# Feed-forward activations transposed by the DMA crossbar as two 16-bit planes instead of by TensorE

## Chip, cores and metric

The kernel runs on one core of a Trainium2 chip. The metric is the device time of one launch in microseconds, the median of several runs. The core has five engines that each take their own instructions in order: TensorE (PE, with its weight loads shown as PEld), VectorE (DVE), ScalarE (ACT), GpSimd (POOL) and SyncE (SP). Sixteen DMA engines move data beside them; in the kernel before, all weight loads are issued from SP.

## What is computed

Two layers of a decoder trunk (sequence 256, model width 2048, float32). Each layer has an attention mixer with an input and an output projection, and then a gated feed-forward block. Only the last matters here:

```python
def swiglu(xn, w_gate, w_up, w_down):
    return (jax.nn.silu(xn @ w_gate) * (xn @ w_up)) @ w_down   # 2048 -> 5632 -> 2048

# per layer
xn = rms_norm(h, norm_ffn[layer])
h = h + swiglu(xn, w_gate[layer], w_up[layer], w_down[layer])
```

## The kernel before

**Precision.** A float32 product is made from three float32r products: each operand is split into a high part (a copy rounded to float32r) and a low part (the rest), and `mm` runs the passes high x high, low x high, high x low, for two row tiles of 128 tokens each.

**Items.** The weights stream through as a list of items, 402 for each layer. Nearly every item is a 128 x 1024 float32 tile (512 KB): two k-steps of 128 rows by 512 columns. In the feed-forward block an item is 2 k-steps x 3 passes x 2 row tiles = 12 matmuls of 512 columns. For an item, SP loads `raw`, ACT copies it to `hi`, DVE subtracts to get `lo`. There are five `raw` buffers and four each of `hi` and `lo`. In the loop, item i first runs `step(active)` (one step of every live side task, a Python generator that issues some instructions and yields), then `prefetch(i)`, which issues the split of item i+3 and the loads up to five items beyond it, and then the matmuls of item i. So the order of instructions on each engine is written out by this loop: whatever a side task issues in its k-th step stands ahead of the split of that turn.

**Feed-forward order.** The hidden width is cut into 11 chunks of 512 columns. The first part takes chunks 0 to 5, the second chunks 6 to 10. For each chunk come 8 items of `w_gate` (`g`) and 8 of `w_up` (`u`). After the `g` items `silu` runs as a side task, after the `u` items `gated`. When the chunks of a part are done, four `w_down` groups (`d0` to `d3`) multiply the transposed activations of that part: 12 items each in the first part, 10 in the second. The items of a group take the chunks in order, two items for each chunk, so in the second part the last chunk, 10, is first used by the ninth item of `d0`; in the first part chunk 5 is first used by the eleventh.

**The side task `gated`.** Counting from the last `u` item of the chunk, its steps fall in the turns of the following items, called item 1, item 2 and so on here. Step 1 (DVE) multiplies the silu tile `sil` by the second accumulator. Steps 2 and 3, one row tile each, run four TensorE transposes of 128 x 128 into a PSUM tile, a copy on ACT to `ah` (high part) and a subtraction on DVE to `al` (low part). Then the pair is put into `act[c]`, from which the `w_down` matmuls take their stationary operand. If the loop comes to a matmul whose `act[c]` isn't set yet, it runs further steps at once, behind the split of that turn:

```python
src = act if it.mat == "w_down" else XF
for kt in it.kts:
    while src[kt // 4] is None:
        step(active)
mm(pos, accs, lambda kt: src[kt // 4])
```

Of the kernel before, what the change touches and what calls it, by code (L numbers as in the profile page):

```python
# [6 lines left out]

F32 = mybir.dt.float32
F32R = mybir.dt.float32r
I32 = mybir.dt.int32  # L10
AF = mybir.ActivationFunctionType
OP = mybir.AluOpType
AX = mybir.AxisListType.X

P = 128
D = 2048
S = 256
# [104 lines left out]
def trunk(ctx: ExitStack, tc: tile.TileContext, x, positions, cst, gT, gfin, bgate, posT, w2, ws, out):  # L122
    nc = tc.nc
    V, A, T = nc.vector, nc.scalar, nc.tensor
# [14 lines left out]
    def tmp_ps():  # L139
        return ps.tile([P, 512], F32, tag="t", name="tps", bufs=3)  # L140
# [18 lines left out]
    def split_next():  # L159
        i = ptr[1]  # L160
        n = seq[i][1].n
        r = raw.pop(i)
        hi, lo = places[i]() if i in places else (wp.tile([P, 1024], F32R, tag="hi", name="hi", bufs=4),
                                                  wp.tile([P, 1024], F32R, tag="lo", name="lo", bufs=4))
        A.activation(hi[:, :n], r[:, :n], AF.Copy)  # L165
# [41 lines left out]
    w2t = cp.tile([P, DEPTH, 2, 2, P], F32, name="w2t")  # L207
    posi = cp.tile([P, 3], I32, name="posi")
    h = hp.tile([P, 2, D], F32, name="h")

    ident = cs[:, C_ID:C_ID + P]
# [150 lines left out]
    def xt_alloc(X, c):  # L362
        X[c] = (xp.tile([P, 4, S], F32R, tag="xh", name="xh", bufs=5),
                xp.tile([P, 4, S], F32R, tag="xl", name="xl", bufs=5))

# [74 lines left out]
    for l in range(DEPTH):  # L440
        g_mix, g_grp, g_ffn = gt[:, 3 * l, :], gt[:, 3 * l + 1, :], gt[:, 3 * l + 2, :]
        flags.clear()
        with ExitStack() as actx:
# [44 lines left out]
            def c_chunk(which, accs):  # L488
# [28 lines left out]
                while which == "cv" and "wk" not in flags:  # L517
                    yield
                fr = ap.tile([P, 32, 60], F32R, tag="fr", name="fr", bufs=1)
                for a in range(2):  # L520
# [293 lines left out]
            while seq[pos][1].mat in ("w_in", "w_cmp_k1", "w_cmp_v1"):  # L814
# [9 lines left out]
                if it.mat == "w_in":  # L824
# [14 lines left out]
                    if it.name == "sv1" and it.kts[-1] in (3, 7, 11):  # L839
                        c = it.kts[-1] // 4  # L840
# [34 lines left out]
            while seq[pos][1].mat == "w_out":  # L875
# [12 lines left out]
                c = int(it.name[1])  # L888
# [9 lines left out]
        with ExitStack() as fctx:  # L898
            fp = fctx.enter_context(tc.tile_pool(name=f"fp{l}", bufs=1))
            r = norm.r  # L900
            act = [None] * NFF
            sil = {}
# [8 lines left out]
                yield  # L911

            def gated(c, accs):
                for t in range(2):
                    s = sil[c, t]
                    V.scalar_tensor_tensor(s, accs[t], r[:, t:t + 1], s, op0=OP.mult, op1=OP.mult)  # L916
                yield
                ah = fp.tile([P, 4, S], F32R, tag="ah", name="ah", bufs=6)
                al = fp.tile([P, 4, S], F32R, tag="al", name="al", bufs=6)
                for t in range(2):  # L920
                    s = sil[c, t]
                    pt = tmp_ps()
                    for j in range(4):
                        T.transpose(pt[:, j * P:(j + 1) * P], s[:, j * P:(j + 1) * P], ident)  # L924
                    sl = slice(t * P, t * P + P)
                    pv = pt.rearrange("p (a b) -> p a b", a=4)
                    A.activation(ah[:, :, sl], pv, AF.Copy)  # L927
                    V.tensor_tensor(al[:, :, sl], pv, ah[:, :, sl].bitcast(F32), op=OP.subtract)  # L928
                    yield
                act[c] = (ah, al)  # L930

            last = l == DEPTH - 1
# [36 lines left out]
            while pos < (end_at if last else len(seq)) and seq[pos][1].mat in ("w_gate", "w_up", "w_down"):  # L969
                it = seq[pos][1]  # L970
                step(active)
                prefetch(pos)
                if it.first:
                    accs = [acc(), acc()]
# [5 lines that stand above are left out]
                if it.last:  # L980
                    c = int(it.name[1:])
                    if it.mat == "w_down":
                        end = it.k1 == KFF
                        spawn(d_add(accs, c, end, norm))
                        if end and not last:
                            spawn(xt_gen(X, c, lambda t, c=c: h[:, t, quad(c)], gt[:, 3 * (l + 1), :], f"d{c}"))
                    else:
                        spawn(silu(c, accs) if it.mat == "w_gate" else gated(c, accs))
                parts.pop(pos)
                pos += 1  # L990
# [94 lines left out]
```

## Time and profile before

| | us |
|---|---|
| median of 3 runs (2310.41 to 2310.79) | 2310.58 |
| the profiled execution's own time | 2310.39 |
| its span from first to last instruction | 2308.6 |
| TensorE busy in the span | 2290.6 |
| DVE busy | 1330.4 |
| ACT busy | 1078.9 |

The profiled execution's time is its span and 1.8 us around it. Busy time of TensorE counts a matmul from its start to its modelled end, and successive matmuls overlap; what a matmul costs in the stream is read from the distance between starts.

### The profile page before, as it was taken

Reading aid. Unit: us, or ns where it says so; the run is one execution under the profiler, and the core shown is the slowest. Engines: PE = TensorE matmul, PEld = TensorE weight load, DVE = VectorE, ACT = ScalarE, POOL = GpSimd, SP = SyncE. Lnnn points to the kernel's source line nnn. Section 1 sums busy time; section 2 is a strip of 40 time slices with the busy share of each in tenths; the row PEclk is TensorE's granted clock in tenths of the full one; section 3 lists DMA queues with packets and bytes.
Section 4 is the critical chain, followed back from the end, with each engine's and each line's share of the span. In section 5 each row is a group of like instructions: output and inputs, shape, how many; then the busy total and the mean of one; then the engine's idle time right before and its main releaser. Section 6 shows DMA issues by size and latency. Waiting matters only on the chain.

```text
span 2308.6 us, 28280 instructions
## 1 busy us (share of the span) xinstructions
PE 2290.6 (99%) x10842; PEld 1906.9 (83%) x10842; DVE 1330.4 (58%) x1766; ACT 1078.9 (47%) x1405; POOL 28.7 (1%) x59
## 2 busy tenths in 40 slices
PE   8999999999999999999999999999999999999998
PEld 7888888888888888888888888888888888888886
DVE  6766776655445445445567667765544544444554
ACT  6645554544444344444455455544444433444443
POOL 4000000000000000000000000000000000000000
PEclk9999999999999999999999999999999999999999
DMA  7854456566666666666567434456556565555653
GB/s 250 277 169 128 128 156 198 181 187 190 189 192 190 194 192 184 192 191 189 178 215 252 147 133 142 157 187 206 186 186 196 183 196 196 186 192 189 190 191 137
DMA packets 118824, 428.46 MB, mean 186 GB/s; under 512 B 13424, under 2 KB 13840, under 8 KB 118560
## 3 DMA queue, kind: packets, MB, share of 16 engines
q1 hardware_dynamic: 118464, 426.58, 58.3%
q8 instruction: 85, 1.39, 0.2%
q14 instruction: 51, 0.42, 0.0%
q0 software_dynamic: 224, 0.07, 0.0%
HBM read 424.50 MB, written 2.10 MB: 185 GB/s over the span
## 4 chain that ended last, share of the span: by engine, by line
PE 98%; DVE 1%; ACT 1%; DMA 0%; SPq 0%; issue 0%; ACTq 0%
PE acc L408 90%; PE ops L669 1%; PE tps L640 1%; PE tps L924 1%; PE tps L373 1%; PE ops L538 1%; PE ops L539 1%; PE tps L615 1%; PE tps L661 0%; PE ops L796 0%; DMA h<-in_x_dram 0%; PE tps L763 0%; PE ops L703 0%; PE tps L678 0%; DVE c L772 0%; DVE lo L166 0%
## 5 line engine op out<-in xcount | busy, mean ns | idle before, releaser
L166 DVE TENSOR_TENSOR lo<-raw,hi 128x1024 fp32r<-128x1024 f32 (+1 forms) x798 | 970.2, 1220 | 782.2 <-ACT hi L165 778.6
L165 ACT ACTIVATE hi<-raw 128x1024 fp32r<-128x1024 f32 (+1 forms) x798 | 836.2, 1054 | 779.7 <-PE acc L408 768.0
L408 PE MATMUL acc<-hi,xh 128*128 128x512 f32 (+2 forms) x2432 | 758.6, 393 | 0.0
L408 PE MATMUL acc<-hi,xl 128*128 128x512 f32 (+2 forms) x2432 | 739.2, 385 | 0.0
L408 PE MATMUL acc<-lo,xh 128*128 128x512 f32 (+2 forms) x2432 | 737.2, 384 | 0.0
L408 PEld LDWEIGHTS acc<-lo,xh 128*128 128x128 f32 x2432 | 453.2, 188 | 92.9 <-DVE lo L166 0.2
L408 PEld LDWEIGHTS acc<-hi,xl 128*128 128x128 f32 x2432 | 453.3, 188 | 92.4
L408 PEld LDWEIGHTS acc<-hi,xh 128*128 128x128 f32 x2432 | 442.6, 189 | 84.3 <-issue 6.7
L408 PE MATMUL acc<-hi,ah 128*128 128x512 f32 x680 | 211.6, 391 | 0.0
L408 PE MATMUL acc<-hi,al 128*128 128x512 f32 x680 | 210.8, 389 | 0.0
L408 PE MATMUL acc<-lo,ah 128*128 128x512 f32 x680 | 210.7, 389 | 0.0
L408 PEld LDWEIGHTS acc<-lo,ah 128*128 128x128 f32 x680 | 127.7, 188 | 26.7
L408 PEld LDWEIGHTS acc<-hi,al 128*128 128x128 f32 x680 | 127.6, 188 | 26.6
L408 PEld LDWEIGHTS acc<-hi,ah 128*128 128x128 f32 x680 | 126.8, 188 | 25.6
L927 ACT ACTIVATE ah<-tps 128x512 fp32r<-128x512 f32 x44 | 26.3, 598 | 92.3 <-PE tps L924 92.3
L928 DVE TENSOR_TENSOR al<-tps,ah 128x512 fp32r<-128x512 f32 x44 | 30.4, 691 | 54.8 <-ACT ah L927 54.8
L380 ACT ACTIVATE xh<-scr 128x512 fp32r<-128x512 f32 x48 | 29.2, 630 | 44.4 <-DVE scr L375 44.4
L909 ACT ACTIVATE sil<-acc,nr 128x512 f32<-128x512 f32 x44 | 27.9, 686 | 38.9 <-PE acc L408 38.9
L663 ACT ACTIVATE pT<-tps 128x256 f32<-128x256 f32 (+1 forms) x32 | 15.7, 491 | 63.2 <-PE tps L661 63.2
L375 DVE TENSOR_TENSOR scr<-tps,gt 128x512 f32<-128x512 f32 x48 | 30.9, 684 | 23.3 <-PE tps L373 23.3
L916 DVE SCALAR_TENSOR_TENSOR sil<-acc,nr,sil 128x512 f32<-128x512 f32 x44 | 31.0, 747 | 13.9 <-PE acc L408 13.9
L383 DVE TENSOR_TENSOR xl<-scr,xh 128x512 fp32r<-128x512 f32 x48 | 31.3, 692 | 5.0 <-ACT xh L380 2.9
(197 smaller groups left out, 976.0 us busy)
## 6 DMA issues: line engine op xcount, KB each, us to landing
raw<-in_ws_dram SPq DMA_DIRECT2D x792, 512.0 KB, 4.1
raw<-in_ws_dram SPq DMA_DIRECT2D x10, 420.0 KB, 4.8
h<-in_x_dram SPq DMA_DIRECT2D x3, 512.0 KB, 8.2
gf<-in_gfin_dram SPq DMA_DIRECT2D x1, 1024.0 KB, 6.6
out_dram<-h SPq DMA_DIRECT2D x4, 256.0 KB, 2.3
out_dram<-h SPq DMA_DIRECT2D x2, 512.0 KB, 3.1
cs<-in_cst_dram SPq DMA_DIRECT2D x1, 802.0 KB, 5.8
h<-in_x_dram SPq DMA_DIRECT2D x2, 256.0 KB, 4.0
```

The costliest lines, as they stand in the source:

```text
L165: A.activation(hi[:, :n], r[:, :n], AF.Copy)
L166: V.tensor_tensor(lo[:, :n], r[:, :n], hi[:, :n].bitcast(F32), op=OP.subtract)
L373: T.transpose(pt[:, j * P:(j + 1) * P], src[:, j * P:(j + 1) * P], ident)
L375: V.tensor_tensor(tv, pt.rearrange("p (a b) -> p a b", a=4), g[:, 4 * c:4 * c + 4, None].to_broadcast([P, 4, P]), op=OP.mult)
L380: A.activation(xh[:, :, t * P:t * P + P], ts[t], AF.Copy)
L383: V.tensor_tensor(xl[:, :, sl], ts[t], xh[:, :, sl].bitcast(F32), op=OP.subtract)
L408: T.matmul(accs[t][:, :it.w], x_[:, kt % 4, t * P:t * P + P], w_[:, sl], start=(kt == it.k0 and n == 0), stop=(kt == it.k1 - 1 and n == 2))
L538: T.matmul(o[:60, :256], fr[:, kt, :], hi[:, sl], start=(kt == 0), stop=False)
L909: A.activation(s, accs[t], AF.Silu, scale=r[:, t:t + 1])
L916: V.scalar_tensor_tensor(s, accs[t], r[:, t:t + 1], s, op0=OP.mult, op1=OP.mult)
L927: A.activation(ah[:, :, sl], pv, AF.Copy)
L928: V.tensor_tensor(al[:, :, sl], pv, ah[:, :, sl].bitcast(F32), op=OP.subtract)
```

## The change

The four TensorE transposes per row tile go, and with them the PSUM tile. Instead ACT takes each float32 tile apart into its two 16-bit halves (`pl`, 128 x 1024 of uint16 for each row tile), one transposing DMA issued from ACT moves all of `pl` (128 x 2048 of uint16, 512 KB, as sixteen 128 x 128 blocks) into `plt`, ACT puts the halves together again in `sT` by four copies, and then one ACT copy and one DVE subtraction of 128 x 1024 make `ah` and `al`. `pl`, `plt` and `sT` have one buffer each. The task has 10 yields where it had 3.

```diff
             def gated(c, accs):
                 for t in range(2):
                     s = sil[c, t]
                     V.scalar_tensor_tensor(s, accs[t], r[:, t:t + 1], s, op0=OP.mult, op1=OP.mult)
                 yield
+                pl = fp.tile([P, 2, 2, 512], U16, tag="pl", name="pl", bufs=1)
+                for t in range(2):
+                    A.activation(pl[:, t], sil[c, t].bitcast(U16).rearrange("p (n b) -> p b n", b=2), AF.Copy)
+                    yield
+                pt = fp.tile([P, 2, 2, 512], U16, tag="plt", name="plt", bufs=1)
+                nc.scalar.dma_start(pt.rearrange("p t b (a s) -> p (t b a) s", a=4),
+                                    pl.rearrange("p t b n -> p (t b n)"), transpose=True)
+                for _ in range(4):
+                    yield
+                f = fp.tile([P, 4, S], F32, tag="sT", name="sT", bufs=1)
+                fv = f.rearrange("p a s -> p (a s)").bitcast(U16).rearrange("p (a t s b) -> p t b a s", a=4, t=2, b=2)
+                for t in range(2):
+                    for b in range(2):
+                        A.activation(fv[:, t, b], pt[:, t, b].rearrange("p (a s) -> p a s", a=4), AF.Copy)
+                    yield
                 ah = fp.tile([P, 4, S], F32R, tag="ah", name="ah", bufs=6)
                 al = fp.tile([P, 4, S], F32R, tag="al", name="al", bufs=6)
-                for t in range(2):
-                    s = sil[c, t]
-                    pt = tmp_ps()
-                    for j in range(4):
-                        T.transpose(pt[:, j * P:(j + 1) * P], s[:, j * P:(j + 1) * P], ident)
-                    sl = slice(t * P, t * P + P)
-                    pv = pt.rearrange("p (a b) -> p a b", a=4)
-                    A.activation(ah[:, :, sl], pv, AF.Copy)
-                    V.tensor_tensor(al[:, :, sl], pv, ah[:, :, sl].bitcast(F32), op=OP.subtract)
-                    yield
+                A.activation(ah, f, AF.Copy)
+                V.tensor_tensor(al, f, ah.bitcast(F32), op=OP.subtract)
+                yield
                 act[c] = (ah, al)
```

Every line number of the kernel rises by 1 ahead of this place and by 11 behind it.

On ACT, around the first chunk of layer 0, before (`hi<-raw` is the split of an item, `sil<-acc,nr` the silu of a chunk, x9 means nine in a row):

```order
L909 ACTIVATE sil<-acc,nr 128x512 x2
L165 ACTIVATE hi<-raw 128x1024 x9
L927 ACTIVATE ah<-tps 128x4x128
L165 ACTIVATE hi<-raw 128x1024
L927 ACTIVATE ah<-tps 128x4x128
L165 ACTIVATE hi<-raw 128x1024 x6
L909 ACTIVATE sil<-acc,nr 128x512 x2
```

And the same place now:

```order
L910 ACTIVATE sil<-acc,nr 128x512 x2
L166 ACTIVATE hi<-raw 128x1024 x9
L923 ACTIVATE pl<-sil 128x1024
L166 ACTIVATE hi<-raw 128x1024
L923 ACTIVATE pl<-sil 128x1024
L166 ACTIVATE hi<-raw 128x1024
L926 DMA_TRANSPOSE plt<-pl 128x16x128
L166 ACTIVATE hi<-raw 128x1024 x4
L934 ACTIVATE sT<-plt 128x4x128 x2
L166 ACTIVATE hi<-raw 128x1024
L934 ACTIVATE sT<-plt 128x4x128 x2
L910 ACTIVATE sil<-acc,nr 128x512 x2
```

The two short copies have become two long ones, a DMA issue, and, four splits later, two pairs of short ones; the `ah` copy follows after one more split, behind the next chunk's silu.

Around the last chunk (10) of layer 0, ACT now has, with buffer numbers (`hi_8376` is the split of the item that first needs chunk 10, `hi_8435` that of the item three later):

```order
L166 ACTIVATE hi_8376<-raw_8283 128x1024
L166 ACTIVATE hi_8394<-raw_8305 128x1024
L934 ACTIVATE sT_8412<-plt_8338 128x4x128 x2
L166 ACTIVATE hi_8415<-raw_8324 128x1024
L934 ACTIVATE sT_8412<-plt_8338 128x4x128 x2
L166 ACTIVATE hi_8435<-raw_8344 128x1024
L938 ACTIVATE ah_8441<-sT_8412 128x1024
L166 ACTIVATE hi_8457<-raw_8362 128x1024
```

On PE the matmuls at the border between the item before and that item now read:

```order
L409 MATMUL acc_8285<-lo_8359,ah_8147 128x512
L409 MATMUL acc_8286<-lo_8359,ah_8147 128x512
L409 MATMUL acc_8285<-hi_8376,ah_8441 128x512
L409 MATMUL acc_8286<-hi_8376,ah_8441 128x512
L409 MATMUL acc_8285<-hi_8376,al_8442 128x512
L409 MATMUL acc_8286<-hi_8376,al_8442 128x512
```

And on DVE the subtractions around `al` of that chunk:

```order
L167 TENSOR_TENSOR lo_8416<-raw_8324,hi_8415 128x1024
L167 TENSOR_TENSOR lo_8436<-raw_8344,hi_8435 128x1024
L939 TENSOR_TENSOR al_8442<-sT_8412,ah_8441 128x1024
L167 TENSOR_TENSOR lo_8458<-raw_8362,hi_8457 128x1024
```

So `ah` and `al` of chunk 10 stand behind the split `hi_8435`/`lo_8436`, which is issued in the same turn as the matmuls that need them.

## Rows read from the trace of the kernel before

**Rows 1.** The page: span, busy time by engine, the chain that ended last.

```profile
span 2308.6 us, 28280 instructions
PE 2290.6 (99%) x10842; PEld 1906.9 (83%) x10842; DVE 1330.4 (58%) x1766; ACT 1078.9 (47%) x1405; POOL 28.7 (1%) x59
...
PE 98%; DVE 1%; ACT 1%; DMA 0%; SPq 0%; issue 0%; ACTq 0%
PE acc L408 90%; PE ops L669 1%; PE tps L640 1%; PE tps L924 1%; PE tps L373 1%; PE ops L538 1%; PE ops L539 1%; PE tps L615 1%; PE tps L661 0%; PE ops L796 0%; DMA h<-in_x_dram 0%; PE tps L763 0%; PE ops L703 0%; PE tps L678 0%; DVE c L772 0%; DVE lo L166 0%
```

**Rows 2.** Groups by line: busy us, mean ns of one, idle before and releaser.

```profile
L166 DVE TENSOR_TENSOR lo<-raw,hi 128x1024 fp32r<-128x1024 f32 (+1 forms) x798 | 970.2, 1220 | 782.2 <-ACT hi L165 778.6
L165 ACT ACTIVATE hi<-raw 128x1024 fp32r<-128x1024 f32 (+1 forms) x798 | 836.2, 1054 | 779.7 <-PE acc L408 768.0 <-DMA raw<-in_ws_dram 4.4 <-PE ops L538 2.3
...
L408 PEld LDWEIGHTS acc<-hi,ah 128*128 128x128 f32 x680 | 126.8, 188 | 25.6
...
L380 ACT ACTIVATE xh<-scr 128x512 fp32r<-128x512 f32 x48 | 29.2, 630 | 44.4 <-DVE scr L375 44.4
...
L927 ACT ACTIVATE ah<-tps 128x512 fp32r<-128x512 f32 x44 | 26.3, 598 | 92.3 <-PE tps L924 92.3
L924 PE MATMUL tps<-cs,sil 128*128 128x128 f32 x176 | 26.3, 272 | 0.0
```

**Rows 3.** Timeline of PE around chunk 0, layer 0: start, us, instruction.

```profile
473.66 0.60 PE L924 MATMUL tps<-cs,sil 128*128 128x128 f32 x4
474.01 0.70 PE L408 MATMUL acc<-hi,xh 128*128 128x512 f32 x2
474.55 0.63 PE L408 MATMUL acc<-hi,xl 128*128 128x512 f32 x2
...
476.85 0.60 PE L924 MATMUL tps<-cs,sil 128*128 128x128 f32 x4
```

**Rows 4.** Timeline of ACT, chunks 9 and 10 of layer 0; brackets: idle before.

```profile
1005.17 0.60 ACT L927 ACTIVATE ah<-tps 128x512 fp32r<-128x512 f32 x1 [2.55 <-PE tps L924]
...
1018.84 1.06 ACT L165 ACTIVATE hi<-raw 128x1024 fp32r<-128x1024 f32 x1 [1.66 <-PE acc L408]
1021.56 1.06 ACT L165 ACTIVATE hi<-raw 128x1024 fp32r<-128x1024 f32 x1 [1.66 <-PE acc L408]
1024.51 1.27 ACT L909 ACTIVATE sil<-acc,nr 128x512 f32<-128x512 f32 x2 [1.89 <-PE acc L408]
...
1049.65 0.60 ACT L927 ACTIVATE ah<-tps 128x512 fp32r<-128x512 f32 x1 [2.55 <-PE tps L924]
```

**Rows 5.** Timelines of ACT, DVE and PE where `d0` reaches chunk 10, layer 0.

```profile
1068.76 1.06 ACT L165 ACTIVATE hi<-raw 128x1024 fp32r<-128x1024 f32 x1 [1.66 <-PE acc L408]
...
1069.86 1.23 DVE L166 TENSOR_TENSOR lo<-raw,hi 128x1024 fp32r<-128x1024 f32 x1 [1.50 <-ACT hi L165]
...
1069.02 0.62 PE L408 MATMUL acc<-hi,ah 128*128 128x512 f32 x2
1069.47 0.61 PE L408 MATMUL acc<-hi,al 128*128 128x512 f32 x2
1069.92 0.62 PE L408 MATMUL acc<-lo,ah 128*128 128x512 f32 x2
```

**Rows 6.** The page: DMA queue (last: share of 16 engines); issues, KB, us to landing.

```profile
q1 hardware_dynamic: 118464, 426.58, 58.3%
...
raw<-in_ws_dram SPq DMA_DIRECT2D x792, 512.0 KB, 4.1
...
out_dram<-h SPq DMA_DIRECT2D x2, 512.0 KB, 3.1
...
gt<-in_gT_dram SPq DMA_DIRECT2D x1, 48.0 KB, 2.9
```

**Rows 7.** Windows after the last matmul: busy us by engine, granted clock, DMA share, GB/s.

```profile
2302.00:2304.00 2.00, 0.00 (x0) 0.00 (x0) 1.72 (x6) 1.20 (x3) 0.00 (x0) 1.00 0.00 0
2304.00:2306.00 2.00, 0.00 (x0) 0.00 (x0) 0.06 (x1) 0.25 (x1) 0.00 (x0) 0.72 0.89 342
```

More of the change, by code (lines that the diff above doesn't have):

```diff
@@ L9 @@
 F32R = mybir.dt.float32r
+U16 = mybir.dt.uint16
 I32 = mybir.dt.int32
```

## Prediction

> **What bounds the kernel.** I began with the page: TensorE is busy for 99% of the span, and the chain that ended last lies on it for 98% [rows 1]. The next question is whether anything else is near. The groups by line say no: ACT's splits take 1.05 us each and stood idle for 768 us in all until a matmul freed their buffer, and DVE's subtractions waited for ACT [rows 2]. So the weights are always split well ahead, and a change pays one for one if it takes time out of TensorE's stream, and costs nothing on ACT or DVE until it makes TensorE wait.
>
> How much ahead, the timeline shows. One feed-forward item lasts 2.72 us (the distance of two splits, 1018.84 to 1021.56) [rows 4]; in each, ACT works 1.06 us and idles 1.66. The split that runs as item k starts is for item k+3; it begins 0.26 us ahead of item k's first matmul (1068.76 against 1069.02) [rows 5].
>
> **What goes.** Four transposes: from the start of one such group to the next, with twelve 512-column matmuls between, it is 473.66 to 476.85, 3.19 us where an item alone is 2.72 [rows 3, 4]. So a group costs 0.47 to 0.48 us. The mean of 272 ns in the group's row would say 1.09, but these overlap [rows 2]. A check over a whole chunk: the same ACT copy comes 44.48 us later in the next chunk (1005.17, 1049.65), and 16 items are 43.52 [rows 4], so 0.96 us for each chunk's two groups. There are 176 transposes, 44 groups, 22 chunks: 22 x 0.96 = 21.1 us. All of it lies on TensorE, the path; the full sum counts.
>
> **What comes on ACT.** For each chunk: two copies of 128 x 1024 into `pl`, four of 128 x 512 into `sT`, one of 128 x 1024 into `ah`, against two copies of 0.60 that go. No row has a 16-bit copy. The nearest rows by elements are 1.05 us for 128 x 1024 and 0.60 to 0.63 for 128 x 512 [rows 2]; I take these: 3 x 1.05 + 4 x 0.6 - 1.2 = 4.4 us more in a chunk of 43.5 us in which ACT idles over 20. Lower bound: half of that, for half the bytes; upper bound: twice, since every second 16-bit element is touched. Either is hidden under idle time of ACT, item by item: the fullest turn has two short copies, two silus (1.27) and a split, 3.6 us against 2.72, and the split has nearly 7 us in hand. DVE gives up two subtractions and gets one of 1.22: nothing.
>
> **The DMA.** The transposing DMA is issued right behind the split that runs as item 3 starts, and ACT's first copy that needs it stands behind the split of item 7: four items, 10.9 us, later. Behind that copy on ACT stand the splits. How late could it land without loss? Take any chunk but 5 and 10. If the first copy starts late by x, the chain copy pair, split, copy pair, two silus, split gives the second split (for item 12) finished about 3.9 + x after item 8 starts, and it must be done some 0.5 us before item 12 starts, 10.3 after: x up to 6.5 us. So the free time from issue to use is 10.9 us, and up to 17.4 before TensorE waits.
>
> What does it take? No row shows a transposing DMA. Below, a 512 KB store took 3.1 us and a 512 KB load 4.1 [rows 6]; at zero it can't be, since the bytes must move. Above: if the sixteen 128 x 128 blocks were served one after another at the price of a small DMA of its own, 2.9 us for 48 KB [rows 6], it would be 16 x 2.9 = 46 us. I take about 5 us, near the load, as it is one instruction with the bytes of one load. Then it is hidden. The engines' bytes: one more 512 KB transfer on sixteen loads; a load is issued five items (13.6 us) before its split and lands in 4.1, so it can lose 9 us unseen. If ACT is held while it issues the transpose, even for 4 us, that is made up within three items' idle time.
>
> The Trainium skill (Advanced Engine Details and Errata, X-Bar Transpose) says that such transposes run about as fast as ordinary DMAs, at 350 to 400 GB/s; by it, 512 KB would be some 1.4 us and a latency. By that the term is zero too; no row here shows it.
>
> **What is late next.** The task now has 10 yields, so `act[c]` is set in turn 11. For chunks inside a part nobody asks. Chunk 5 is first used in item 11: its `ah` and `al` are issued a turn earlier and are some 2.4 us early. Chunk 10 is first used in item 9: there the loop finds `act[10]` unset after the split of that turn has been issued, so `ah` stands on ACT behind the split for item 12, and `al` on DVE behind its subtraction. That split can't start before item 8's matmuls have freed its buffer. In the times of layer 0: split 1068.76 to 1069.82, `ah` (1.05) to 1070.9, `lo` 1069.86 to 1071.09 [rows 5], `al` (1.22) to 1072.3. The first pair, due at 1069.02, starts near 1071.1 (behind `ah` and a weight load of 0.19 [rows 2]), stands again, and the `al` pair, due at 1069.47, starts near 1072.5. TensorE loses 3.1 us, in both layers: 6.2 us. The granted clock stays at 1.00 (2.4 GHz) until more than 4 us after the last matmul and falls only then [rows 7], so waits of 2 us and 1 us should not lower it.
>
> **Sum.** Against the profiled execution's own 2310.4 (0.2 below the median): 2310.4 - 21.1 + 6.2 = 2295.5 us.
>
> **Rivals.**
> *The transpose lands too late (slower).* With x the lateness beyond 10.9 us, chunk 10 loses x - 0.4 more in each layer (0.4 us is what ACT has idle there between the second copy pair and the split for item 12), chunk 5 loses x - 2.8 (its 2.4 and that 0.4), the 18 others x - 6.5. The gain of 14.9 is eaten when 2(x - 0.4) + 2(x - 2.8) = 14.9, x = 5.3: 16 us from issue to landing decides. Beyond 17.4 each further us costs 22. At the upper bound of 46 us (x = 35.5) it is 70 + 65 + 522 = 657 us on top, some 2950 us. For it: sixteen blocks in one instruction, 2-byte elements, and DMA engines that are already 58% busy [rows 6]. Against: rows of the same bytes land in 3 to 4 us [rows 6]. Chance 0.07.
>
> The Trainium skill (VectorE: DVE Perf Modes, The three transpose paths) speaks against the change: it gives 1309 ns for one 128 x 128 block by DMA against 390 by TensorE, and advises TensorE where the result may go to PSUM. If the blocks ran one after another at that price, an estimate of 21 us would come out, x = 10, and about 2395 us; in this trace TensorE's block costs 0.12 us of stream, so by both it is dear there only if it isn't hidden.
>
> *It eats the gain.* The same mechanism with 15 to 17.4 us: within 0.2% of before, 2306 to 2315 us. It needs a landing four times as slow as the loads. Chance 0.05.
>
> *No stall at chunk 10.* If the order cost nothing there, 2289.3 us. Against: the order of instructions says it plainly. Chance 0.08.
>
> *The removal itself* can't fail: no transposes of `sil` are left on TensorE.
>
> **Chances and range.** The forecast has 0.80. It would be 2289.3 without stalls, 2298.5 if the 16-bit copies cost double (then chunk 10 loses 1.5 us more in each layer), and 2303 if the DMA lands 2.8 us late. I give 2289 to 2304. A measurement of this kernel tells some 0.2% (4.6 us) from no change. Faster: 0.80 + 0.08 = 0.88; same 0.05; slower 0.07.
>
> **What would show it.** In the profile after: no `sil` transposes on TensorE; chunk to chunk 43.5 us instead of 44.48; one wait of 2 us for ACT and one of about 1 us for DVE in each layer, where `d0` reaches chunk 10, and no other new wait of TensorE; the DMA landing less than 10.9 us after its issue, with ACT's `sT` copies not waiting for it. I am wrong if ACT stands waiting for the DMA at `sT` and its splits come late, if the loads of `raw` land so late that ACT waits for them, or if TensorE's pace of 2.72 us an item changes.

## Result and profile after

The changed kernel takes 2295.31 us (median, 2295.05 to 2296.56) against 2310.49 for the kernel before on the same chip: ratio 0.9936, 95% interval 0.9923 to 0.9948, faster by 15.2 us. The forecast was 2295.5. The span fell from 2308.6 to 2293.4 [rows 1].

The page of the changed kernel, with its busy times and the two hardware DMA queues (q1 carries the loads from SP, q10 is new; columns: packets, MB, share of 16 engines):

```profile
span 2293.4 us, 28108 instructions
PE 2269.5 (99%) x10666; PEld 1888.1 (82%) x10666; DVE 1322.7 (58%) x1744; ACT 1176.6 (51%) x1515; POOL 28.7 (1%) x59
...
q1 hardware_dynamic: 118464, 426.58, 58.4%
q10 hardware_dynamic: 45760, 11.54, 3.1%
```

TensorE has 176 instructions fewer, ACT works 98 us more, and TensorE is still busy for 99%. The groups by line that are new or whose waits changed (the first two stood at 0.0 idle before):

```profile
L409 PE MATMUL acc<-hi,ah 128*128 128x512 f32 x680 | 211.1, 390 | 3.3 <-ACT ah L938 3.3
L409 PE MATMUL acc<-hi,al 128*128 128x512 f32 x680 | 211.0, 389 | 1.4 <-DVE al L939 1.4
...
L934 ACT ACTIVATE sT<-plt 128x512 uint16<-128x512 uint16 x88 | 61.7, 766 | 0.0
...
L923 ACT ACTIVATE pl<-sil 128x1024 uint16<-128x1024 uint16 x44 | 46.2, 1050 | 0.0
```

A new wait of TensorE for ACT and one for DVE, and ACT's first use of the transposed data has no idle time ahead of it: the DMA was always there. The timeline of ACT where `d0` comes to chunk 10 in layer 0, then DVE and PE at the same place; it answers to [rows 5]:

```profile
1056.32 1.41 ACT L934 ACTIVATE sT<-plt 128x512 uint16<-128x512 uint16 x2
1058.07 1.06 ACT L166 ACTIVATE hi<-raw 128x1024 fp32r<-128x1024 f32 x1 [0.35 <-PE acc L409]
1059.03 1.04 ACT L938 ACTIVATE ah<-sT 128x1024 fp32r<-128x1024 f32 x1
...
1059.16 1.22 DVE L167 TENSOR_TENSOR lo<-raw,hi 128x1024 fp32r<-128x1024 f32 x1 [1.49 <-ACT hi L166]
1060.30 1.22 DVE L939 TENSOR_TENSOR al<-sT,ah 128x1024 fp32r<-128x1024 f32 x1
...
1057.87 0.61 PE L409 MATMUL acc<-lo,ah 128*128 128x512 f32 x2
1060.12 0.73 PE L409 MATMUL acc<-hi,ah 128*128 128x512 f32 x2 [1.64 <-ACT ah L938]
1061.58 0.73 PE L409 MATMUL acc<-hi,al 128*128 128x512 f32 x2 [0.72 <-DVE al L939]
1062.14 0.63 PE L409 MATMUL acc<-lo,ah 128*128 128x512 f32 x2
1062.61 0.62 PE L409 MATMUL acc<-hi,ah 128*128 128x512 f32 x2
1063.07 0.62 PE L409 MATMUL acc<-hi,al 128*128 128x512 f32 x2
```

Read it as one chain: the split for item 12 (1058.07) starts when a buffer comes free, `ah` follows it, `lo` and then `al` follow on DVE, and the two pairs of matmuls wait for one after the other. Pairs come every 0.453 us in the steady stream (2.72 us for six, [rows 4]), so the pairs behind 1057.87 were due at 1058.32, 1058.78, 1059.23, 1059.68 and 1060.14. They started at 1060.12, 1061.58, 1062.14, 1062.61 and 1063.07: 1.80, 2.80, 2.91, 2.93 and 2.93 late. The loss is 2.9 us, once in each layer.

### The profile page after: what moved, and what is told of

Read it like the earlier page. It is cut to its first block, busy times and chain, and to the rows that moved or that the text cites. A ratio compares the mean times of both kernels' runs of the same rounds, so it can differ in the third digit from the quotient of the medians.

```text
span 2293.4 us, 28108 instructions
## 1 busy us (share of the span) xinstructions
PE 2269.5 (99%) x10666; PEld 1888.1 (82%) x10666; DVE 1322.7 (58%) x1744; ACT 1176.6 (51%) x1515; POOL 28.7 (1%) x59
## 3 DMA queue, kind: packets, MB, share of 16 engines
q1 hardware_dynamic: 118464, 426.58, 58.4%
q10 hardware_dynamic: 45760, 11.54, 3.1%
## 5 line engine op out<-in xcount | busy, mean ns | idle before, releaser
L934 ACT ACTIVATE sT<-plt 128x512 uint16<-128x512 uint16 x88 | 61.7, 766 | 0.0
L923 ACT ACTIVATE pl<-sil 128x1024 uint16<-128x1024 uint16 x44 | 46.2, 1050 | 0.0
```

What stands on the lines that cost most here:

```text
L923: A.activation(pl[:, t], sil[c, t].bitcast(U16).rearrange("p (n b) -> p b n", b=2), AF.Copy)
L934: A.activation(fv[:, t, b], pt[:, t, b].rearrange("p (a s) -> p a s", a=4), AF.Copy)
```

## Experiments

All changes are to the changed kernel unless it is said otherwise. One number in the task `gated` was the handle for most of them: the count of yields between the transposing DMA and its first use. It sets both how long the DMA has and whether chunk 10's `ah` is issued ahead of the split in the turn that needs it.

For gap3 (gap2, gap1 and gap0 have 2, 1 and 0 in its place, gap5 and gap6 further down 5 and 6):

```diff
-                for _ in range(4):
+                for _ in range(3):
                     yield
                 f = fp.tile([P, 4, S], F32, tag="sT", name="sT", bufs=1)
```

**gap3.** 

> Three yields instead of four between the transposing DMA and its first use; the task has 9 yields, so the ah copy of chunk 10 is issued in the ninth item's turn ahead of the split for item 12. Order theory (the changed kernel loses about 2.95 us in each layer because ah and al of chunk 10 stand behind a split that can't start yet, and nothing else is lost): about 0.3 us of the wait is left in each layer, 2290.0 us (2289.3 to 2291). Contention theory (the roughly 6 us that the change gives back are spread over all 22 transposing DMAs, which slow the stream or the splits): no change, 2295 us.

**gap2.** 

> Two yields: 5.4 us from issue to first use, against landings of 5.3 to 9.6 us in the changed kernel, so ACT now waits for the DMA in most chunks. Order theory with the slack that was worked out (ACT may be some 6 us late before TensorE notices): both waits at chunk 10 gone, 2289.4 us (2289 to 2290). Contention theory: 2295 us. A theory by which ACT's waiting for the DMA costs TensorE at once: 22 x 2 us more, above 2330 us.

**gap1.** 

> One yield: 2.7 us from issue to first use; ACT waits some 4.7 us, at most 7. Slack theory: a wait up to about 6 us is free, so 2289.5 us, up to 2293 if some landings come after 9 us. If the slack were only the three items' idle time of ACT (5 us): some 2295 to 2300 us.

**gap0.** 

> No yield: the first use stands right behind the DMA's issue on ACT, which waits the whole landing, 5.3 to 9.6 us, 7.4 in the middle. By the slack theory TensorE loses what a landing takes beyond 7.1 us: about 0.8 us a chunk, 2307 us (2297 to 2315). If the slack is larger than worked out: 2289.5 us. If ACT's waiting were not hidden at all: above 2400 us.

| yields | median us | ratio to before, 95% interval |
|---|---|---|
| 4 (the change) | 2295.31 | 0.9936, 0.9923 to 0.9948 |
| 3 | 2289.76 | 0.9910, 0.9895 to 0.9925 |
| 2 | 2289.29 | 0.9908, 0.9893 to 0.9923 |
| 1 | 2289.57 | 0.9909, 0.9895 to 0.9924 |
| 0 | 2291.51 | 0.9919, 0.9902 to 0.9936 |

With two yields TensorE has no wait left for `ah` or `al`, and 6 us come back; with three about 0.2 us is left in each layer, where 0.3 was expected. With two, ACT already waits for the DMA in 19 of 22 chunks, 22.4 us in all, and nothing is lost:

```profile
L409 PE MATMUL acc<-hi,ah 128*128 128x512 f32 x680 | 210.9, 389 | 0.0
...
L934 ACT ACTIVATE sT<-plt 128x512 uint16<-128x512 uint16 x88 | 61.9, 769 | 22.4 <-DMA plt<-pl 22.4
```

So the order of the instructions and not the DMA cost the 6 us. Contention is out, since the DMAs are all still there. With one yield ACT waits 61.0 us in all, and 2289.57 is what the slack theory gave. With no yield ACT waits 145.1 us in all, up to 8.2 at a time, and the time rises by only 2.2 us: I had expected some 17. In the profiled execution three chunks make it up: where the first use came 8.68, 8.80 and 9.27 us after the issue, the next chunk came 0.48, 0.59 and 1.07 us late; where it came within 8.2 us, next to nothing was lost. One chunk of gap0 that lost nothing, with the DMA's issue on ACT's own queue (ACTq) and the wait behind it:

```profile
520.54 1.06 ACT L166 ACTIVATE hi<-raw 128x1024 fp32r<-128x1024 f32 x1 [0.71 <-ACT pl L923]
520.57 4.25 ACTq L926 DMA_TRANSPOSE plt<-pl  x1
528.28 1.41 ACT L934 ACTIVATE sT<-plt 128x512 uint16<-128x512 uint16 x2 [6.67 <-DMA plt<-pl]
529.55 1.03 ACT L166 ACTIVATE hi<-raw 128x1024 fp32r<-128x1024 f32 x1
```

The issue stands behind the split in the order, but begins 0.03 us after it and runs beside it: I had placed it 1.03 us later, at the split's end. And copies and splits that follow at once overlap a little (529.55 starts before 528.28 + 1.41 ends). So there was more slack than I had worked out; gap0twice below measures it.

**removed.** The kernel before, without the transposes of `sil` on TensorE.

```diff
-                    pt = tmp_ps()
-                    for j in range(4):
-                        T.transpose(pt[:, j * P:(j + 1) * P], s[:, j * P:(j + 1) * P], ident)
                     sl = slice(t * P, t * P + P)
-                    pv = pt.rearrange("p (a b) -> p a b", a=4)
+                    pv = s.rearrange("p (a b) -> p a b", a=4)
```

> The removal alone: the kernel before without the TensorE transposes of sil; ah and al are taken from the untransposed sil (so the down projection multiplies untransposed activations), three yields as before, no DMA and no 16-bit copies. The sum's first term says 22 x 0.96 = 21.1 us less than before: 2289.4 us. If the transposes' cost in the stream overlaps with something, less: 2292 to 2300 us.

2289.37 us, ratio 0.9909 (0.9894 to 0.9924); the span is 2287.6, 21.0 below before. The first term of the sum is as large as forecast, and gap2 (2289.29) gets all of it.

**added.** The kernel before with the new path beside the old one, its result unused.

```diff
+                pl = fp.tile([P, 2, 2, 512], U16, tag="pl", name="pl", bufs=1)
...
                     V.tensor_tensor(al[:, :, sl], pv, ah[:, :, sl].bitcast(F32), op=OP.subtract)
+                    A.activation(pl[:, t], s.bitcast(U16).rearrange("p (n b) -> p b n", b=2), AF.Copy)
                     yield
                 act[c] = (ah, al)
+                pt = fp.tile([P, 2, 2, 512], U16, tag="plt", name="plt", bufs=1)
+                nc.scalar.dma_start(pt.rearrange("p t b (a s) -> p (t b a) s", a=4),
+                                    pl.rearrange("p t b n -> p (t b n)"), transpose=True)
...
+                A.activation(ah2, f, AF.Copy)
```

> The additions alone: the kernel before with its TensorE transposes, and beside them the whole new path (two 16-bit copies, the transposing DMA, four copies, one long copy) whose result is not used. Order theory: all of it is hidden, 2310.5 us (2310 to 2311.5). Contention theory: about 6 us slower, 2316 us.

2310.41 us, ratio 1.0001 (0.9992 to 1.0010). Everything that was added is hidden.

**twice.** Each transposing DMA is issued twice.

```diff
+                for k in range(1):
+                    px = fp.tile([P, 2, 2, 512], U16, tag=f"px{k}", name=f"px{k}", bufs=1)
+                    nc.scalar.dma_start(px.rearrange("p t b (a s) -> p (t b a) s", a=4),
+                                        pl.rearrange("p t b n -> p (t b n)"), transpose=True)
                 nc.scalar.dma_start(pt.rearrange("p t b (a s) -> p (t b a) s", a=4),
```

> The changed kernel with each transposing DMA issued twice, first into a scratch tile that nobody reads. The one that is needed lands about one sequencer hold later (3.6 us), 9 to 13 us after the first issue, where the first use comes at 10.9. Slack theory: only chunk 10 feels it, by 0 to 2 us in each layer, 2295.5 to 2299 us. If the DMA engines' time is what costs: 6 us more than the changed kernel, 2301 us.

2297.10 us (2295.37 to 2297.95), ratio 0.9945 (0.9928 to 0.9961). In the profiled execution (span 2293.6) TensorE's waits are those of the changed kernel, 3.3 us for `ah` and 1.4 for `al`, and no `sT` copy waited: a second 512 KB of transposing in every chunk costs next to nothing there. Behind chunk 9 of layer 0 TensorE is 0.4 us late: that chunk's two issues hold ACT's queue for 9.7 us, and the splits behind them start late:

```profile
998.41 4.51 ACTq L928 DMA_TRANSPOSE px<-pl  x1
1002.95 5.20 ACTq L930 DMA_TRANSPOSE plt<-pl  x1
1008.25 3.90 ACT L166 ACTIVATE hi<-raw 128x1024 fp32r<-128x1024 f32 x4 [8.80 <-issue]
```

The medians differ by 1.8 us all the same. The three slower executions have mean clocks of 0.998, 0.997 and 0.998 where the profiled one has 0.999. A fall of the clock as in gap5 below would fit; no trace of these executions shows it.

**gap5 and gap6.** More yields push `sT` copies behind the split too.

> Five yields: a longer way from the DMA to its first use, so no landing can matter. In chunk 10 the second pair of sT copies too now stands behind the split for item 12, ahead of ah. Order theory: the wait grows from 2.95 by a copy pair (1.27 us) to 4.2 us in each layer, and chunk 5 begins to lose 0.2: 2289.3 + 8.4 + 0.4 = 2298.1 us (2297 to 2299). A theory by which landings cost: no change or better than 2295 us.

> Six yields: in chunk 10 all four sT copies and ah stand behind the split for item 12, and in chunk 5 ah stands behind the split of the turn that first needs it. Order theory: chunk 10 loses 5.5 us and chunk 5 2.95 us in each layer, 2289.3 + 11.0 + 5.9 = 2306.2 us (2304 to 2308). Landing theory: 2295 us or less.

gap5 took 2301.55 us, ratio 0.9964 (0.9951 to 0.9977); gap6 2311.17, ratio 1.0005 (0.9996 to 1.0014), so the whole gain is gone. The direction is the order theory's, and the landing theory is out, since these give the DMA most time. But both are above my figures, by 3.4 and 5 us. The timeline of PE in gap5 at chunk 10, layer 0:

```profile
1058.00 0.61 PE L409 MATMUL acc<-lo,ah 128*128 128x512 f32 x2
1061.68 0.73 PE L409 MATMUL acc<-hi,ah 128*128 128x512 f32 x2 [3.07 <-ACT ah L938]
1062.94 0.73 PE L409 MATMUL acc<-hi,al 128*128 128x512 f32 x2 [0.53 <-DVE al L939]
1063.51 0.82 PE L409 MATMUL acc<-lo,ah 128*128 128x512 f32 x2
1064.13 1.05 PE L409 MATMUL acc<-hi,ah 128*128 128x512 f32 x2
1064.98 1.05 PE L409 MATMUL acc<-hi,al 128*128 128x512 f32 x2
...
1068.30 0.62 PE L409 MATMUL acc<-hi,ah 128*128 128x512 f32 x2
```

And windows of the same stretch (busy us and count of PE, PEld, DVE, ACT and POOL, then granted clock, DMA share, GB/s):

```profile
1060.00:1062.00 2.00, 0.32 (x1) 0.30 (x2) 0.85 (x2) 1.60 (x2) 0.00 (x0) 1.00 0.77 221
1062.00:1064.00 2.00, 1.48 (x6) 0.93 (x5) 0.89 (x1) 0.00 (x0) 0.00 (x0) 0.95 0.53 203
1064.00:1066.00 2.00, 2.00 (x6) 1.52 (x6) 0.00 (x0) 0.00 (x0) 0.00 (x0) 0.50 0.02 8
1066.00:1068.00 2.00, 2.00 (x8) 1.58 (x7) 0.84 (x1) 1.06 (x1) 0.00 (x0) 0.70 0.00 0
```

After the wait of 3.07 us the granted clock falls to 0.50 (1.2 GHz) with TensorE at work again, and pairs come every 0.85 us instead of 0.453. The pair at 1068.30 is the tenth behind 1058.00, due at 1058.00 + 10 x 0.453 = 1062.53: 5.8 us late, where 4.2 were expected; the 1.6 us between are the price of the low clock. In layer 1 the same wait of 3.07 us is followed by the same fall, and the stretch from chunk 10's first `pl` copy to the end is 6.6 us longer than in gap2 (123.67 against 117.06), 2.4 more than expected. Together these 4.0 us are what the profiled execution lies above the figure (2301.99 against 2298.1). In gap6 the wait at chunk 10 is 4.30 us in each layer and the clock falls to 0.50 as well; the stretches from there on are 7.8 and 7.5 us longer than in gap2, where 5.5 were expected. Chunk 5 now has the waits that chunk 10 had, 1.64 and 0.72, and loses 2.97 us in each layer, as expected.

**gap0twice.** No yield, and the DMA twice.

> No yield, and each transposing DMA issued twice, the first into a scratch tile that nobody reads: the needed one lands about 1.4 us later than with no yield alone, some 8.3 us after the first issue (6.5 to 10.7). Lateness law (beyond about 8.3 us each microsecond of lateness costs TensorE one microsecond in that chunk): a loss of about 0.6 us a chunk, 2302 us (2294 to 2312). If lateness were absorbed further: 2291.5 us, as with no yield alone.

2326.60 us (2320.85 to 2332.87), ratio 1.0070 (1.0047 to 1.0094): slower than before, and by more than expected, since the landing that matters came 8.9 to 12.1 us after the first issue in the first six chunks, and not 8.3. The law itself is read chunk by chunk from the timeline of ACT in layer 0 (first DMA, second DMA, first use):

```profile
476.41 1.42 ACTq L928 DMA_TRANSPOSE px<-pl  x1
477.86 7.42 ACTq L930 DMA_TRANSPOSE plt<-pl  x1
487.23 1.39 ACT L938 ACTIVATE sT<-plt 128x512 uint16<-128x512 uint16 x2 [9.78 <-DMA plt<-pl]
522.52 3.95 ACTq L928 DMA_TRANSPOSE px<-pl  x1
526.50 3.11 ACTq L930 DMA_TRANSPOSE plt<-pl  x1
531.65 1.41 ACT L938 ACTIVATE sT<-plt 128x512 uint16<-128x512 uint16 x2 [8.09 <-DMA plt<-pl]
566.96 1.33 ACTq L928 DMA_TRANSPOSE px<-pl  x1
...
655.82 1.33 ACTq L928 DMA_TRANSPOSE px<-pl  x1
657.18 8.80 ACTq L930 DMA_TRANSPOSE plt<-pl  x1
667.91 1.39 ACT L938 ACTIVATE sT<-plt 128x512 uint16<-128x512 uint16 x2 [11.05 <-DMA plt<-pl]
705.47 4.15 ACTq L928 DMA_TRANSPOSE px<-pl  x1
```

Chunk 0: first use 10.82 us after the issue, and the next chunk comes 46.11 us later, 2.59 over the 43.52 of 16 items. Chunk 1: 9.13 us, and 44.44, 0.92 over. Both give 8.2 us free, and each microsecond beyond costs one. Chunk 4: 12.09 us, and 49.65, 6.1 over; the law says 3.9. There TensorE waited 3.21 us and the clock fell to 0.50 again, which is the rest. Of the 20 chunks other than the two chunks 10, all but two give 8.2 (8.18 to 8.23); the other exception is chunk 9 of layer 0, with a wait of 3.54 us and a clock that fell to 0.50, 1.5 us over the law.

## Why the prediction was right

**What goes: right.** 21.1 us were forecast. In the changed kernel a chunk follows the next at 43.52 us (`pl` copies at 993.80 and 1037.32), 0.96 less than before [rows 4], and the removal alone measured 21.0 of span.

```profile
993.80 1.06 ACT L923 ACTIVATE pl<-sil 128x1024 uint16<-128x1024 uint16 x1
...
1037.32 1.06 ACT L923 ACTIVATE pl<-sil 128x1024 uint16<-128x1024 uint16 x1
```

**What comes on ACT: hidden, as forecast, at partly other prices.** The copies into `pl` took 1.05 us as the rows of float copies said; those into `sT` took 0.77, not 0.60 [rows 2]. ACT's busy time still rose by the 4.4 us a chunk of the sum (97.7 in all), because instructions that follow one another at once overlap: a pair of 0.77 takes 1.40. So the sum came out by two errors that cancel. The kernel with the additions alone shows that it made no difference.

**The DMA: mis-sized, and harmless.** About 5 us were taken; it landed after 7.4 in the middle (5.3 to 9.6), below the 10.9 of the four yields (the first use came 11.8 us after the issue). The tile's own view in the changed kernel:

```profile
L926 ACTq DMA_TRANSPOSE plt<-pl x22: 1333/3644/4919, 476.1 to 2177.8; - x22
...
DMA to landing us min/median/max: 5.3/7.4/9.6
```

It is nearly twice the landing of a load of the same 512 KB (3.9 us in this execution), so the near price that I chose, the row of an ordinary load, was too low. About half of it, 3.6 us in the middle, is the time in which the issue holds ACT's queue, which the prediction had allowed for up to 4 us; from the end of that hold it is 3.6 us to the landing. The Trainium skill (Advanced Engine Details and Errata, X-Bar Transpose) says that such a transpose runs about as fast as an ordinary DMA; counted from the issue it is not as fast here, but with the hold in it the landing alone does not decide on the rate. The sixteen blocks do not queue at the price of single small DMAs, the upper bound of 46 us: 7.4 / 16 is 0.46 us a block.

**What is late next: right.** 3.1 us in each layer were forecast, 2.9 measured; it went when chunk 10's `ah` was issued ahead of the split (gap3, gap2), and grew when more was put behind it (gap5, gap6). 21.0 - 2 x 2.9 = 15.2 is the difference of the spans.

**The late transpose: the mechanism is real, and its threshold was too near.** I gave 17.4 us from issue to landing until an ordinary chunk loses. gap0 and gap0twice put it at 8.2 with no yield. Four yields give four items, 10.9 us, more, but they also put the next chunk's two silus ahead of the second split. In twice, at chunk 9 of layer 0, that split ended 5.65 us after the first use (1012.06 to 1017.71) and the first one 2.31 after it; the second has one item, 2.72 us, more time, so it takes some 0.6 us of the slack. That makes about 18.5 us, an estimate: no run had a landing that late with four yields. The step at fault was the issue's time on ACT, 1 us too late. That this beats the kernel before only as long as the landing is hidden is shown by gap0twice, at 2326.6.

**The clock: right for this wait, and close.** In the changed kernel's profiled execution it stays at 1.00 through the waits:

```profile
1058.00:1060.00 2.00, 0.48 (x3) 0.06 (x1) 0.84 (x1) 1.93 (x2) 0.00 (x0) 1.00 0.54 152
1060.00:1062.00 2.00, 1.16 (x4) 0.68 (x5) 1.52 (x2) 0.07 (x1) 0.00 (x0) 1.00 0.74 186
1062.00:1064.00 2.00, 2.00 (x11) 1.60 (x9) 0.00 (x0) 0.27 (x1) 0.00 (x0) 1.00 0.54 209
```

The sign that this was drawn from, a clock at 1.00 until more than 4 us after the last matmul [rows 7], does not carry over to every wait in the stream: in gap5 the clock was at 0.50 after one of 3.07 us. One of the changed kernel's four runs took 2296.56 us at a mean clock of 0.998. That the clock fell there after one of the same waits fits the size, but no trace of that run shows it.

**The range: two of its sums are off.** By the prediction's own law a DMA 2.8 us late costs 2 x 2.4 = 4.8 us, which makes 2300.3; 2303 comes out only with the copies at double price as well. And x = 10 gives about 2392, not 2395. Neither touches the forecast.

## What to carry over

Taking transposes off a saturated TensorE pays their distance in the stream (0.12 us each here), not their listed duration (0.27), if the detour is hidden; whether it is hidden is asked once for each consumer, and the one with the shortest notice decides. Where side tasks are stepped by a loop, count the steps to the first consumer: one yield too many put a ready tile behind a split that could not start, and cost over a quarter of the gain (6 of 21 us). Two yields fewer give 2289.29 us, better than both kernels (0.9908, 0.9893 to 0.9923).

## Not expected of the hardware

- The transposing DMA holds ACT's queue for 1.3 to 4.9 us (3.6 in the middle) after its issue, against 0.4 us for a store's issue on SP at the end of the kernel before. In chunk 9 of layer 0 of the changed kernel it was issued at 998.30 and held the queue for 4.92 us; the next split, due near 1001.0, started at 1003.32. The DMA moved 252 bytes a packet (11.54 MB in 45760), and took 3.1% of the engines' time where the loads took 58.4% for 37 times the bytes: about twice the engine time for a byte.
- A DMA issue that stands behind an ACTIVATE on ACT starts beside it: 0.03 us after that one's start in all 22 chunks of the changed kernel.
- Waits of TensorE of 1.64 and 0.72 us, and in gap0twice of up to 2.04, left the granted clock at 1.00 in the profiled executions. With waits of 3.07 (gap5), 3.21 and 3.54 (gap0twice) and 4.30 us (gap6) it fell to 0.50, at times shortly before the matmuls resumed (1.3 us in gap0twice's chunk 4) and at times after (2.1 us in layer 0 of gap5). In gap5 and gap0twice that cost 1.5 to 2.4 us on top of the wait.
